# Three 256-column matmuls everywhere instead of one of 512 and one of 256, and every activation tile at 192 over a multiple of 256 bytes

## The chip, the cores and the metric

One of the eight cores of a Trainium2 chip runs the whole program. The metric is device time in microseconds (us), from three runs of the kernel before: 1252.30, 1252.81 and 1257.68 us, median 1252.81 us.

## What is computed

One decoder block on 256 tokens of width 2048, in float32. Cut to what matters here, all of its matrix products are:

```python
proj = rms_norm(x) @ w_in + b_in                 # 2048 -> q 1024, k 128, v 128, u 512, two gates of 2048
attn = sliding_window_attention(q, k, v, sinks)  # 16 heads
ssm  = glu(gelu(s5_ssm(u)) @ w_glu + b_glu)      # 512 -> 1024 -> 512
merged = sigmoid(gate_attn) * (attn @ w_branch_attn) + sigmoid(gate_ssm) * (ssm @ w_branch_ssm)
x = x + merged @ w_out                           # 2048 -> 2048
val, gate = split(rms_norm(x) @ w_up)            # 2048 -> 2 * 5632
x = x + (val * gelu(causal_conv(gate))) @ w_down # 5632 -> 2048
return rms_norm(x)
```

## The kernel before

Activations lie transposed: features on the 128 partitions, the 256 tokens along the free axis. Weights stream from memory in 416 units of 512 KB (128 partitions by 1024 floats), one after the other in the order of the blocks: q, u, kv, q, then the gates (ga, gs), the attention output (A), the GLU (glu), the branch of the state-space part (S), the output product (o), 22 blocks of the up-projection (up0 to up21) and 4 of the down-projection (dn0 to dn3). A block makes four output chunks of 128 features (m = 4) over K chunks of 128 input features; K is 16 for ga, gs, o and up, 8 for A, 4 for glu and S, 44 for dn. With m = 4 a unit holds two k steps.

**Precision by two pieces.** Weights and activations are each split into a high piece in the matmul's reduced float32 format (F32R) and a rest, also F32R. A product is made of hi*hi + hi*lo + lo*hi. `prep` does this for a unit: ScalarE casts the raw weights to `whi`, VectorE subtracts to get `wlo`. It runs five units ahead of TensorE (`LOOK`), into five buffers of each kind; four raw buffers are loaded by SyncE's queue.

**Two forms of the product.** For one weight chunk the blocks up to up0, and dn3, issue three matmuls of 256 columns: `whi` by the high activations, `whi` by the low ones, `wlo` by the high ones, all added in the same 256 columns of PSUM. Every matmul instruction loads its own weights. The blocks up1 to up21 and dn0 to dn2 (`double`) issue two: `whi` by high and low activations side by side, 512 columns into 512 columns of PSUM, and `wlo` by the high ones into the first 256. The two halves of the accumulator are added when the block is emptied: `whole` copies the second half to SBUF (ScalarE) and adds the first (VectorE), twice in each of the 21 blocks; `ev_dn` does the same twice in each of three blocks.

**Where the moving operands lie.** Each product streams an activation tile through TensorE. The tiles' addresses within a partition follow from the pools in the order in which they are opened. In the program that is built, the first tile of each kind starts at these places, given as the rest over 256 bytes:

| tile | used by | before | after the change |
|---|---|---|---|
| `A` as `xg`, later `x2g` (2048 bytes for each k: high, then low) | q, u, kv, ga, gs; up | 192 | 192 |
| `ath`, `atl` | A | 0 | 192 |
| `su` | glu | 0 | 192 |
| `sy` | S | 224 | 192 |
| `mh`, `ml` | o | 0 | 192 |
| `H` (2048 bytes for each k: high, then low) | dn | 0 | 192 |
| `whi`, `wlo` (weights) | all | 0 | 0 |

All their steps are whole multiples of 256 bytes, so the rest holds for every matmul of a block.

**What sets the order.** The kernel writes one order per engine by hand. Side work (state-space scan, attention, normalisations) stands in generators that `fill` advances when running tallies of estimated nanoseconds for each engine (`clk_pe`, `clk_v`, `clk_a`) say that there is room. TensorE's part of it (`later`) is put between the matmuls of a block by `run_aux`: attention scores, transposes and values (tile `at`), the state-space products (`pq`, `yp`), sums for the normalisations (`at<-ones,..`, `at<-dg,ones`). From ga to the A blocks there are several dozen such insertions; from the last part of A (A3y) to up0 there is none, in up0 there are two, and from up1 to the tail of dn3 there is none.

Of the kernel before, what the change touches and what calls it, by code (L numbers as in the profile page):

```python
# [8 lines left out]
F32 = mybir.dt.float32  # L9
F32R = mybir.dt.float32r  # L10
I32 = mybir.dt.int32
AF = mybir.ActivationFunctionType
ALU = mybir.AluOpType
AX = mybir.AxisListType

P = 128
T = 256
NK = 16
# [119 lines left out]
def hybrid_block_kernel(  # L138
# [14 lines left out]
    V, S = Counted(nc.vector, clk_v, dve_ns), Counted(nc.scalar, clk_a, act_ns)  # L153
    PE = Counted(nc.tensor, clk_pe, pe_ns)

    base = ctx.enter_context(tc.tile_pool(name="base", bufs=1))
# [3 lines left out]
    def open_pool(name, **kw):  # L160
        cm = tc.tile_pool(name=name, **{"bufs": 1, **kw})
        return cm, cm.__enter__()
# [20 lines left out]
    A = base.tile([P, NK, 2, T], F32R, tag="A", name="xg")  # L183
    Ah, Al = A[:, :, 0], A[:, :, 1]
    mid_cm, mid = open_pool("mid")
    X = mid.tile([P, NK, T], F32, tag="tS", name="x_in")
    ath = mid.tile([P, 8, T], F32R, tag="ath", name="ath")
    atl = mid.tile([P, 8, T], F32R, tag="atl", name="atl")
# [68 lines left out]
    def bc(ap, n):  # L257
        return ap.unsqueeze(1).to_broadcast([P, n, ap.shape[-1]])
# [18 lines left out]
        V.tensor_tensor(sq[:, 0:2], sq[:, 0:2], sq[:, 2:4], op=ALU.add)  # L277
        V.tensor_tensor(sq[:, 0], sq[:, 0], sq[:, 1], op=ALU.add)

# [1 line left out]
    V.memset(ones, 1.0)  # L281
    V.memset(eps, EPS)
    S.activation(hb[:, 0:1], eps, AF.Sqrt)
# [10 lines left out]
    warm = bank("at", P)  # L294
    for i in range(WARM):
        PE.matmul(warm, ones, ones, start=True, stop=True)
# [1 line left out]
    st = {}  # L298
    bq8 = base.tile([P, 8], F32, tag="bq8", name="bq8")

# [28 lines left out]
        ks = range(4 * b, 4 * b + 4)  # L329
        ev_proj(f"{n}{b}", acc, dst[:, 4 * b : 4 * b + 4], None, [hb[:, off + i : off + i + 1] for i in ks], AF.Tanh, 0.5)  # L330

# [1 line left out]
    def g_norm1():  # L333
        sq = mid.tile([P, 2, 4, T], F32, tag="tA", name="sq1")
        v = p1.tile([P, 2], F32, tag="sv1", name="sv1")
# [31 lines left out]
        S.copy(rs, ps[1].rearrange("p h t -> p (h t)"))  # L367
        st["rs"] = True

# [1 line left out]
    def g_ssm():  # L371
        sp = p1.tile([P, 22, NJ], F32, tag="sp", name="sp")
        ki = p1.tile([P, NJ], I32, tag="ki", name="ki")
# [252 lines left out]
        y_ev(3)  # L626
        st["y3"] = True

# [1 line left out]
    def g_attn():  # L630
        yield "D", wait_for("kv", "q0")
        qT = st["qT"]
# [88 lines left out]
    def g_norm2():  # L721
        sq, ps = st["sq"], {}
        yield "D", None
        fold(sq)

        def total():
            ps[0] = bank("at", 2)
            for h in range(2):
                PE.matmul(ps[0][:, h : h + 1], sq[:, 0, h * P : (h + 1) * P], ones[:, 0:1], start=True, stop=True)

        def spread():
            ps[1] = bank("at", 2, P)
            for h in range(2):
                PE.matmul(ps[1][:, h], ones, dg[:, h], start=True, stop=True)

        yield "D", later(total)
        n2 = mid.tile([P, 3, 2], F32, tag="ath", name="n2")
        dg = mid.tile([P, 2, P], F32, tag="atl", name="dg2")
        rstd(ps[0], n2[:, 0], n2[:, 1], n2[:, 2])
        for h in range(2):  # L740
            V.tensor_scalar(dg[:, h], ident, n2[:, 2, h : h + 1], None, op0=ALU.mult)
        yield "A", later(spread)
        st["rs2"] = base.tile([P, T], F32, tag="rs", name="rs2")
        S.copy(st["rs2"], ps[1].rearrange("p h t -> p (h t)"))
        close_pool(st["p2cm"])
        close_pool(mid_cm)
        st["ffncm"], fp = open_pool("ffn")
        st["ffn"] = fp
        st["H"] = fp.tile([P, NFF, 2, T], F32R, tag="H", name="H")
        st["gb"] = fp.tile([P, 2, T + 2], F32, tag="gb", name="gb")  # L750
        V.memset(st["gb"][:, :, 0:2], 0.0)
# [114 lines left out]
                                   in1=st["Ah"][:, k].bitcast(F32), op0=ALU.mult, op1=ALU.subtract)  # L866
        squares(d, b)

    def whole(acc, c0, out, name):
        sl = st["ffn"].tile([P, 2, T], F32, tag="xs", name=name, bufs=2)  # L870
        S.copy(sl, acc[:, c0 : c0 + 2, T : 2 * T])
        V.tensor_tensor(out, acc[:, c0 : c0 + 2, 0:T], sl, op=ALU.add)

    def ev_up(j, acc):
        rs2, fp, g = st["rs2"], st["ffn"], st["gb"]
        y = fp.tile([P, 2, T], F32, tag="cy", name=f"cy{j}")
        v = fp.tile([P, 2, T], F32, tag="cv", name=f"cv{j}")
        gd = g[:, :, 2 : T + 2]
        if j:
            whole(acc, 2, gd, f"xg{j}")  # L880
            V.tensor_tensor(gd, gd, bc(rs2, 2), op=ALU.mult)
        else:
            V.tensor_tensor(gd, acc[:, 2:4], bc(rs2, 2), op=ALU.mult)
        for i in range(2):
            c = 2 * j + i
            S.activation(y[:, i], g[:, i, 2 : T + 2], AF.Identity, bias=pcol("cb", c), scale=pcol("cw", 3 * c + 2))
        if j:
            whole(acc, 0, v, f"xv{j}")
            V.tensor_tensor(v, v, bc(rs2, 2), op=ALU.mult)
        else:  # L890
            V.tensor_tensor(v, acc[:, 0:2], bc(rs2, 2), op=ALU.mult)
        for i in range(2):
            c = 2 * j + i
            for tap in (1, 0):
                V.scalar_tensor_tensor(out=y[:, i], in0=g[:, i, tap : T + tap], scalar=pcol("cw", 3 * c + tap),
                                       in1=y[:, i], op0=ALU.mult, op1=ALU.add)
        S.activation(y, y, AF.Gelu)
        V.tensor_tensor(v, v, y, op=ALU.mult)
        split(st["H"][:, 2 * j : 2 * j + 2, 0], st["H"][:, 2 * j : 2 * j + 2, 1], v)

    def ev_dn(b, acc):
        d = st["X"][:, 4 * b : 4 * b + 4]
        V.tensor_tensor(d, d, acc[:, :, 0:T], op=ALU.add)
        for c in (0, 2):
            sl = st["ffn"].tile([P, 2, T], F32, tag="xs", name=f"xd{b}_{c}", bufs=2)
            S.copy(sl, acc[:, c : c + 2, T : 2 * T])
            V.tensor_tensor(d[:, c : c + 2], d[:, c : c + 2], sl, op=ALU.add)
        squares(d, b)
        for k in range(4 * b, 4 * b + 4):
            S.activation(st["xo"][:, k], st["X"][:, k], AF.Identity, scale=G("fin", k))  # L910
# [14 lines left out]
    def evac(name, acc):  # L925
        if name == "u":
            ev_u(acc)
        elif name == "kv":
            ev_kv(acc)
            spawn(g_attn(), dve=5000.0, act=5000.0, first=True)  # L930
        elif name[0] == "q":
            ev_q(int(name[1]), acc)
        elif name[:2] == "ga":
            if st["tA"] is None:
                st["tA"] = mid.tile([P, NK, T], F32, tag="tA", name="tA")
            ev_gate("ga", st["tA"], int(name[2]), 0, acc)
        elif name[:2] == "gs":
            if st["tS"] is None:
                st["tS"] = mid.tile([P, NK, T], F32, tag="tS", name="tS")
            ev_gate("gs", st["tS"], int(name[2]), 16, acc)  # L940
        elif name[0] == "A":
            ev_A(4 * int(name[1]) + (2 if name[-1] == "y" else 0), 2 if len(name) == 3 else 4, acc)
        elif name[0] == "S":
            ev_S(int(name[1]), acc)
        elif name[:3] == "glu":
            if name == "glu0":
                assert not gens and not aux
                close_pool(p1_cm)
                st["p2cm"], st["p2"] = open_pool("p2")
                p2 = st["p2"]  # L950
                st["mh"] = p2.tile([P, NK, T], F32R, tag="mh", name="mh")
                st["ml"] = p2.tile([P, NK, T], F32R, tag="ml", name="ml")
                st["sy"] = base.tile([P, 2, 4, T], F32R, tag="X", name="sy")
            ev_glu(int(name[3]), acc)
        elif name[0] == "o":
            ev_o(int(name[1]), acc)
        elif name[:2] == "up":
            ev_up(int(name[2:]), acc)
        elif name[:2] == "dn":
            ev_dn(int(name[2]), acc)  # L960
# [48 lines left out]
    for i, (name, K, m, k0, kw) in enumerate(units):  # L1009
# [37 lines left out]
        if name == "dn3" and i >= NU - TAIL:  # L1047
            tail.append((k0, hi, lo))
            prep(i + LOOK)
            continue  # L1050
        double = acc.shape[2] == 512 and name != "dn3"
        for kk in range(kw if double else 0):
            k = k0 + kk
            both = (st["A"] if name[0] == "u" else st["H"])[:, k].rearrange("p s t -> p (s t)")
            for c in range(m):
                PE.matmul(acc[:, c], hi[:, kk, c], both, start=k == 0, stop=False, skip_group_check=True)
                PE.matmul(acc[:, c, 0:T], lo[:, kk, c], mh[:, k], start=False, stop=k == K - 1, skip_group_check=True)
        for kk in range(0 if double else kw):
            k = k0 + kk
            for c in range(m):  # L1060
                o = acc[:, c, 0:T]
                first = k == 0 and (c % 2 == 0 or name == "dn3")
                last = k == K - 1
                PE.matmul(o, hi[:, kk, c], mh[:, k], start=first, stop=False, skip_group_check=True)
                PE.matmul(o, hi[:, kk, c], ml[:, k], start=False, stop=False, skip_group_check=True)
                PE.matmul(o, lo[:, kk, c], mh[:, k], start=False, stop=last, skip_group_check=True)
                run_aux()
            if kk == 0:
                fill()
# [21 lines left out]
        if k0 + kw == K and name == "dn2":  # L1091
            spawn(g_pre(), 2)

# [1 line left out]
    Hh, Hl = st["H"][:, :, 0], st["H"][:, :, 1]  # L1095
    Xr, xo, sq = st["X"], st["xo"], st["sq"]
    n3 = st["ffn"].tile([P, 3, 2], F32, tag="cy", name="n3")
# [141 lines left out]
```

## Time and profile before

| what | value |
|---|---|
| runs of the kernel before | 1252.30, 1252.81, 1257.68 us |
| span of the profiled execution (first to last instruction) | 1249.7 us |
| median of the runs less that span | 3.1 us |
| TensorE matmuls busy / weight loads busy | 1235.7 us (99%) / 1125.1 us (90%) |
| VectorE / ScalarE busy | 856.9 us (69%) / 620.0 us (50%) |
| mean granted TensorE clock | 0.996 |

The profiled execution's own time is its span of 1249.7 us and some 3.1 us around it, if it ran like the median. Matmuls overlap in the trace: one is shown as 276 to 284 ns long while the next starts after some 113 to 120 ns. The time that a stream of matmuls takes is therefore read from the distance between starts, or from a piece of the chain of waits divided by the matmuls in it, not from the mean duration of one. A few per cent of matmul records can be missing, so short pieces are read with care.

### The profile page before, as it was taken

To read this page: it belongs to the slowest core of one execution; us is meant where nothing else is said; L and a number is where in the kernel's file an instruction comes from. 1 tells how busy PE (TensorE), PEld (TensorE's weight loads), DVE (VectorE), ACT (ScalarE), POOL (GpSimd) and SP (SyncE) were. 2 spreads that over 40 slices of the span, in tenths; PEclk is the share of its full clock that TensorE was granted. 3 is DMA by queue.
4 is the path that set the end of the run, shared out by engine and by line. 5 is a ranking of instruction groups with operands and counts; after the bars stand their busy time and mean duration, and the time that the engine had idled before them with its cause. 6 is when DMAs were issued, how large, how long until landed. Compare 5 with 4: busy or idle time off the path is not lost.

```text
span 1249.7 us, 20901 instructions
## 1 busy us (share of the span) xinstructions
PE 1235.7 (99%) x8476; PEld 1125.1 (90%) x8476; DVE 856.9 (69%) x1220; ACT 620.0 (50%) x865; POOL 10.4 (1%) x24
## 2 busy tenths in 40 slices
PE   9999999999999999999999999999999999999996
PEld 8999899989999999988888888888888888888996
DVE  7988998989878556567677666676666755454543
ACT  7676555554444445445445454454455534343531
POOL 0000000000000000000000000000000000000000
PEclk9999999999999999999999999999999999999998
DMA  8565444444446654654655646546456475646451
GB/s 315 205 203 185 162 152 162 140 164 169 153 169 227 207 180 163 205 183 152 214 174 179 216 145 216 189 159 222 159 187 214 140 235 165 208 165 208 165 184 68
DMA packets 64896, 228.29 MB, mean 183 GB/s; under 512 B 7648, under 2 KB 9056, under 8 KB 64672
## 3 DMA queue, kind: packets, MB, share of 16 engines
q1 hardware_dynamic: 63648, 223.55, 52.9%
q0 software_dynamic: 1152, 3.41, 0.9%
q8 instruction: 66, 1.08, 0.4%
q14 instruction: 30, 0.25, 0.1%
HBM read 224.31 MB, written 2.10 MB: 181 GB/s over the span
## 4 chain that ended last, share of the span: by engine, by line
PE 98%; DVE 1%; DMA 0%; ACT 0%; SPq 0%; issue 0%; DVEq 0%
PE acc_up L132 40%; PE acc_dn L132 20%; PE acc_o L132 7%; PE acc_gs L132 7%; PE acc_ga L132 7%; PE acc_q L132 3%; PE acc_A L132 3%; PE pq L132 2%; PE at L132 2%; PE acc_u L132 2%; PE acc_S L132 2%; PE yp L132 1%; PE acc_glu L132 1%; PE aux L132 1%; DMA raw<-in_wst_dram 0%; DVE xo_sq L132 0%
## 5 line engine op out<-in xcount | busy, mean ns | idle before, releaser
L132 DVE TENSOR_TENSOR wlo<-raw,whi 128x1024 fp32r<-128x1024 f32 (+2 forms) x421 | 501.4, 1209 | 277.0 <-ACT whi L132 274.0
L132 ACT CAST whi<-raw 128x1024 fp32r<-128x1024 f32 (+2 forms) x421 | 429.5, 1038 | 420.4 <-PE acc_dn L132 111.3
L132 PE MATMUL acc_up<-x2g,whi 128*128 128x512 f32 (+1 forms) x1472 | 497.2, 387 | 0.0
L132 PE MATMUL acc_up<-x2g,wlo 128*128 128x256 f32 x1408 | 395.4, 281 | 0.0
L132 PEld LDWEIGHTS acc_up<-x2g,whi 128*128 128x128 f32 x1472 | 272.1, 188 | 62.4
L132 PEld LDWEIGHTS acc_up<-x2g,wlo 128*128 128x128 f32 x1408 | 264.3, 188 | 0.0
L132 PE MATMUL acc_dn<-H,whi 128*128 128x512 f32 (+1 forms) x856 | 245.9, 355 | 0.0
L132 PE MATMUL acc_dn<-H,wlo 128*128 128x256 f32 x692 | 194.7, 281 | 0.0
L132 PEld LDWEIGHTS acc_dn<-H,whi 128*128 128x128 f32 x856 | 150.4, 189 | 24.8
L132 PEld LDWEIGHTS acc_dn<-H,wlo 128*128 128x128 f32 x692 | 131.3, 190 | 0.0
L132 PE MATMUL acc_gs<-xg,whi 128*128 128x256 f32 x512 | 91.4, 282 | 0.0
L132 PE MATMUL acc_ga<-xg,whi 128*128 128x256 f32 x512 | 91.2, 282 | 0.0
L132 PEld LDWEIGHTS acc_gs<-xg,whi 128*128 128x128 f32 x512 | 77.8, 189 | 2.6 <-issue 1.7
L132 PEld LDWEIGHTS acc_ga<-xg,whi 128*128 128x128 f32 x512 | 77.6, 188 | 2.8 <-issue 2.0
L132 PE MATMUL acc_o<-mh,whi 128*128 128x256 f32 x256 | 72.5, 283 | 0.0
L132 PE MATMUL acc_o<-ml,whi 128*128 128x256 f32 x256 | 72.5, 283 | 0.0
L132 PE MATMUL acc_o<-mh,wlo 128*128 128x256 f32 x256 | 72.5, 283 | 0.0
L132 PE MATMUL acc_gs<-xg,wlo 128*128 128x256 f32 x256 | 71.3, 278 | 0.0
L132 PE MATMUL acc_ga<-xg,wlo 128*128 128x256 f32 x256 | 71.2, 278 | 0.0
L132 PEld LDWEIGHTS acc_o<-ml,whi 128*128 128x128 f32 x256 | 49.2, 192 | 0.0
L132 PEld LDWEIGHTS acc_o<-mh,whi 128*128 128x128 f32 x256 | 49.2, 192 | 0.0
L132 PEld LDWEIGHTS acc_o<-mh,wlo 128*128 128x128 f32 x256 | 49.2, 192 | 0.0
(212 smaller groups left out, 1371.7 us busy)
## 6 DMA issues: line engine op xcount, KB each, us to landing
raw<-in_wst_dram SPq DMA_DIRECT2D x415, 512.0 KB, 4.2
xres<-in_xT_dram POOLq DMA_DIRECT2D x1, 2048.0 KB, 9.9
x_in<-in_xT_dram SPq DMA_DIRECT2D x7, 256.0 KB, 5.9
out_dram<-xo_sq SPq DMA_DIRECT2D x7, 256.0 KB, 2.4
br<-in_ssmb_dram POOLq DMA_DIRECT2D x3, 256.0 KB, 4.2
raw<-in_wst_dram SPq DMA_DIRECT2D x2, 256.0 KB, 3.4
cT<-in_ssmc_dram SPq DMA_DIRECT2D x1, 512.0 KB, 6.3
us<-ul POOLq DMA_DIRECT2D x16, 32.0 KB, 3.1
```

Source lines behind the costliest of these rows:

```text
L132: return fn(*a, **k)
```

## The change

All blocks use three matmuls of 256 columns; the 512-column form, the accumulator's second half in use and its adding-up (`whole`, the loop in `ev_dn`) go away. VectorE now multiplies straight out of PSUM. The PSUM tiles keep their size of one 2 KB bank for each chunk, of which 256 columns are used. Two unused tiles of 48 floats (192 bytes; `room1`, `room2`) open the pools `mid` and `ffn` and so push what follows by 192 bytes; `sy` is cut out of a larger tile 56 floats (224 bytes) behind its start.

```diff
@@ pools
     mid_cm, mid = open_pool("mid")
+    mid.tile([P, 48], F32, tag="room", name="room1")
     X = mid.tile([P, NK, T], F32, tag="tS", name="x_in")
...
         st["ffn"] = fp
+        fp.tile([P, 48], F32, tag="room", name="room2")
         st["H"] = fp.tile([P, NFF, 2, T], F32R, tag="H", name="H")
...
-                st["sy"] = base.tile([P, 2, 4, T], F32R, tag="X", name="sy")
+                sy = base.tile([P, NK * T], F32R, tag="X", name="sy")[:, 56 : 56 + 8 * T]
+                st["sy"] = sy.rearrange("p (s k t) -> p s k t", s=2, k=4)
@@ emptying the accumulators
-    def whole(acc, c0, out, name):
-        sl = st["ffn"].tile([P, 2, T], F32, tag="xs", name=name, bufs=2)
-        S.copy(sl, acc[:, c0 : c0 + 2, T : 2 * T])
-        V.tensor_tensor(out, acc[:, c0 : c0 + 2, 0:T], sl, op=ALU.add)
...
-        if j:
-            whole(acc, 2, gd, f"xg{j}")
-            V.tensor_tensor(gd, gd, bc(rs2, 2), op=ALU.mult)
-        else:
-            V.tensor_tensor(gd, acc[:, 2:4], bc(rs2, 2), op=ALU.mult)
+        V.tensor_tensor(gd, acc[:, 2:4, 0:T], bc(rs2, 2), op=ALU.mult)
...
-        if j:
-            whole(acc, 0, v, f"xv{j}")
-            V.tensor_tensor(v, v, bc(rs2, 2), op=ALU.mult)
-        else:
-            V.tensor_tensor(v, acc[:, 0:2], bc(rs2, 2), op=ALU.mult)
+        V.tensor_tensor(v, acc[:, 0:2, 0:T], bc(rs2, 2), op=ALU.mult)
...
-        for c in (0, 2):
-            sl = st["ffn"].tile([P, 2, T], F32, tag="xs", name=f"xd{b}_{c}", bufs=2)
-            S.copy(sl, acc[:, c : c + 2, T : 2 * T])
-            V.tensor_tensor(d[:, c : c + 2], d[:, c : c + 2], sl, op=ALU.add)
@@ the products
-        double = acc.shape[2] == 512 and name != "dn3"
-        for kk in range(kw if double else 0):
-            k = k0 + kk
-            both = (st["A"] if name[0] == "u" else st["H"])[:, k].rearrange("p s t -> p (s t)")
-            for c in range(m):
-                PE.matmul(acc[:, c], hi[:, kk, c], both, start=k == 0, stop=False, skip_group_check=True)
-                PE.matmul(acc[:, c, 0:T], lo[:, kk, c], mh[:, k], start=False, stop=k == K - 1, skip_group_check=True)
-        for kk in range(0 if double else kw):
+        for kk in range(kw):
             k = k0 + kk
             for c in range(m):
                 o = acc[:, c, 0:T]
-                first = k == 0 and (c % 2 == 0 or name == "dn3")
+                first = k == 0 and (c % 2 == 0 or acc.shape[2] == 512)
                 last = k == K - 1
                 PE.matmul(o, hi[:, kk, c], mh[:, k], start=first, stop=False, skip_group_check=True)
                 PE.matmul(o, hi[:, kk, c], ml[:, k], start=False, stop=False, skip_group_check=True)
```

TensorE's order at the border from up0 to up1, before the change (`acc_up_6054` is up0's accumulator, `acc_up_6341` up1's; `x2` stands for two instructions alike):

```order
L132 MATMUL acc_up_6054<-x2g,whi_6141 128x256 x2
L132 MATMUL acc_up_6054<-x2g,wlo_6142 128x256
L132 MATMUL acc_up_6341<-x2g,whi_6184 128x512
L132 MATMUL acc_up_6341<-x2g,wlo_6185 128x256
L132 MATMUL acc_up_6341<-x2g,whi_6184 128x512
```

And with the change (`acc_up_6343` is up1's):

```order
L132 MATMUL acc_up_6055<-x2g,whi_6142 128x256 x2
L132 MATMUL acc_up_6055<-x2g,wlo_6143 128x256
L132 MATMUL acc_up_6343<-x2g,whi_6185 128x256 x2
L132 MATMUL acc_up_6343<-x2g,wlo_6186 128x256
L132 MATMUL acc_up_6343<-x2g,whi_6185 128x256 x2
```

Each `whi` row of 512 columns becomes two of 256 at the same place, 1344 times in up1 to up21 and 528 times in dn0 to dn2; nothing else changes its place on TensorE.

VectorE where block up1 is emptied, before:

```order
L132 TENSOR_TENSOR gb<-acc_up_6341,xg_6520 128x2x256
L132 TENSOR_TENSOR gb<-gb,rs_6235 128x2x256
L132 TENSOR_TENSOR cv_6519<-acc_up_6341,xv_6526 128x512
L132 TENSOR_TENSOR cv_6519<-cv_6519,rs_6235 128x512
L132 SCALAR_TENSOR_TENSOR cy_6518<-gb,pr,cy_6518 128x256 x4
```

And with the change:

```order
L132 TENSOR_TENSOR wlo_6579<-raw_6462,whi_6578 128x1024
L132 TENSOR_TENSOR gb<-acc_up_6343,rs_6236 128x2x256
L132 TENSOR_TENSOR cv_6585<-acc_up_6343,rs_6236 128x512
L132 SCALAR_TENSOR_TENSOR cy_6584<-gb,pr,cy_6584 128x256 x4
L132 TENSOR_TENSOR cv_6585<-cv_6585,cy_6584 128x512
```

Two of VectorE's instructions go in each block (48 in all with dn0 to dn2), and with them 48 copies on ScalarE (`xg`, `xv`, `xd`). One weight cast of ScalarE changes places with a neighbour; SyncE's and GpSimd's orders stay.

## The prediction

> **What bounds the kernel now.** I read the page's first two parts, then the chain of waits, then the timeline of TensorE in the stages that the change touches.
>
> ```profile
> span 1249.7 us, 20901 instructions
> PE 1235.7 (99%) x8476; PEld 1125.1 (90%) x8476; DVE 856.9 (69%) x1220; ACT 620.0 (50%) x865; POOL 10.4 (1%) x24
> PEclk9999999999999999999999999999999999999998
> PE 98%; DVE 1%; DMA 0%; ACT 0%; SPq 0%; issue 0%; DVEq 0%
> ```
>
> The chain that ended last is TensorE for 98% of the span, at full granted clock. So the time is the number of matmuls times their pace, and only the pace can change it. "99% busy" says nothing of the pace. The chain in order of time does: a piece's time over its count.
>
> ```profile
> 63.03 11.90 PE acc_q L132 x105
> 74.93 0.22 PE at L132 x2
> 75.15 4.24 PE acc_q L132 x36
> 86.46 6.01 PE acc_ga L132 x51
> 363.15 8.64 PE acc_glu L132 x72
> 383.81 11.60 PE acc_S L132 x96
> 395.41 92.15 PE acc_o L132 x768
> 502.60 482.71 PE acc_up L132 x2757
> 985.31 241.27 PE acc_dn L132 x1512
> ```
>
> All the matmuls of the first seven rows but the two of `at` have 256 columns, and there are three paces:
> - **quick**, 113.3 ns: 11.90 / 105 on tile `xg` (192 over 256 bytes);
> - **middle**, 117.8 ns: 4.24 / 36 and 6.01 / 51, same tile, same shape, after two other matmuls came between;
> - **slow**, 120.0 ns: 8.64 / 72 and 92.15 / 768, tiles `su`, `mh`, `ml` (0 over 256).
>
> S, at 224, runs at about 119 (11.60 us less the first one after a stall, over 95, is somewhat above). Nothing but the tile's place separates the 768 matmuls of o from those of q and ga: shape, weights' place and clock are the same. So I read the slow pace as due to place 0, and place 192 as having two paces.
>
> Of the shape that goes, the groups by form give the price:
>
> ```profile
> L132 PE MATMUL acc_up<-x2g,whi 128*128 128x512 f32 x1344 | 474.9, 397 | 0.0
> L132 PE MATMUL acc_dn<-H,whi 128*128 128x512 f32 x528 | 186.6, 399 | 0.0
> ```
>
> One of 512 is shown longer (397 ns) than the distance to the next, so its busy time covers the pair of 512 and 256: 474.9 / 1344 = 353.4 ns, 186.6 / 528 = 353.4 ns. Three of 256 take 340.0 at the quick pace, 353.4 at the middle one and 360.0 at the slow one. **The change gains 13.4 ns for each of 1872 triples at the quick pace, nothing at the middle, and loses 6.6 at the slow.** Each ns of pace is worth 1872 x 3 = 5.6 us.
>
> **Which pace the new stretch gets.** Block up0 already has the new form, on the very tile (`x2g`, 192). Its timeline shows starts of `wlo` matmuls, one for each triple:
>
> ```profile
> 487.99 0.28 PE L132 MATMUL acc_up<-x2g,wlo 128*128 128x256 f32 x1
> 496.49 0.28 PE L132 MATMUL acc_up<-x2g,wlo 128*128 128x256 f32 x1
> 496.60 0.50 PE L132 MATMUL at<-ones,sqA 128*128 128x1 f32 x4
> 497.64 0.28 PE L132 MATMUL acc_up<-x2g,wlo 128*128 128x256 f32 x1
> 501.52 0.28 PE L132 MATMUL acc_up<-x2g,wlo 128*128 128x256 f32 x1
> 502.00 0.27 PE L132 MATMUL at<-dg,ones 128*128 128x128 f32 x1
> 502.68 0.28 PE L132 MATMUL acc_up<-x2g,wlo 128*128 128x256 f32 x1
> 510.16 0.28 PE L132 MATMUL acc_up<-x2g,wlo 128*128 128x256 f32 x1
> ```
>
> Between the first two rows are 25 triples: 8.50 / 75 = 113.3. After the first insertion 11 triples take 3.88 us: 117.6. After the second, 22 triples take 7.48 us: 113.3. So the pace holds while nothing comes between, and each of these two insertions changes it over; the two together leave it as it was. Behind them up1 to the tail of dn3 has no insertion, nor has the way from S to up0. The pace in which S leaves its one stall therefore decides some 850 us:
>
> ```profile
> 381.31 1.22 DVE wlo L132
> 382.53 1.14 DVE tS L132
> 383.67 0.14 issue
> ```
>
> TensorE waits there until VectorE has emptied an accumulator of S. This wait stays; when it ends against TensorE's own beat is not in the profile. I bound the pace by the nearest rows: of the 39 streams of eight or more matmuls on `xg` between two insertions, 22 are quick and 17 middle; the first and last whole pieces are
>
> ```profile
> 12.96 2.72 PE acc_q L132 x24
> 287.71 6.01 PE acc_gs L132 x51
> ```
>
> (113.3 and 117.8). I take quick, by that majority and because up0, the one place where a stream came out of tiles at 0 to a tile at 192, began quick.
>
> **The change part by part**, quick pace, middle in brackets:
> 1. o: 768 x (120.0 - 113.3) = 5.1 us (1.7).
> 2. S: 192 x about 5.6 = 1.1 us (0.2); its stall stays.
> 3. A and glu: 480 matmuls, 3.2 us (1.1). Insertions cut A, so both paces will mix: 2.0 us.
> 4. up0: nothing (0.5 us lost, since its quick and middle stretches, some 147 and 41 matmuls, would change places).
> 5. up1 to up21: 1344 x 13.4 ns = 18.0 us (0).
> 6. dn0 to dn2: 528 x 13.4 ns = 7.1 us (0).
> 7. dn3 with its tail, already three of 256: 176 x 20.0 ns = 3.5 us (1.2).
>
> Sum 36.8 us (3.7). q to gs don't change; their mix of paces is open from run to run, 256 + 256 triples of ga and gs at 13.4 ns being 6.9 us from end to end, which may be why the runs differ by 5.4 us.
>
> 8. The adding-up that goes: 42 + 6 copies on ScalarE and as many additions on VectorE.
>
> ```profile
> L132 ACT COPY xg<-acc_up 128x512 f32<-128x512 f32 x21 | 12.1, 578 | 0.0
> L132 DVE TENSOR_TENSOR cv<-acc_up,xv 128x512 f32<-128x512 f32 x21 | 14.5, 691 | 34.2 <-ACT xv L132 34.2
> ```
>
> Some 27 us of ScalarE and 33 us of VectorE (with `xv`, `xg` and `xd`), all beside TensorE: worth nothing. If TensorE waited for an emptied accumulator they would be worth up to 2.5 us a block, but two accumulators alternate and each has a whole block of 21.7 us.
>
> 9. A quicker TensorE eats a unit of 24 matmuls in 2.72 us instead of 2.83. ScalarE's cast (1.05 us) and VectorE's subtraction (1.22 us) fit, and the supply has been faster:
>
> ```profile
> 10.00:40.00 30.00, 29.80 (x262) 29.80 (x263) 27.88 (x62) 23.83 (x33) 0.00 (x0) 1.00 0.92 339
> 47.00:74.00 27.00, 27.00 (x241) 27.00 (x240) 25.41 (x64) 16.08 (x24) 0.00 (x0) 1.00 0.61 201
> 600.00:980.00 380.00, 380.00 (x2153) 330.05 (x2152) 258.20 (x304) 189.53 (x236) 0.00 (x0) 1.00 0.55 184
> ```
>
> 512 KB in 2.72 us is 193 GB/s; the second row held the quick pace at 201 GB/s with VectorE and ScalarE busier than in up, at clock 1.00. Should a unit come late, the stream would stop and draw its pace anew.
>
> The third weight load in a triple shows in those rows too: weight loads are busy for 330 of 380 us in up and for all of 27 us in q at the quick pace, so they fill TensorE's load side without setting the pace there.
>
> Two rules of the Trainium skill speak against the change. "TensorE: Matmul & The Clock Gate", section Back-to-back issue gap, gives N/2.4 + 2.5 ns a matmul; by that a pair is 325.0 and a triple 327.5 ns, an estimate of 4.7 us more for 1872. The rows disagree: 256 columns never took less than 113.3 ns. The same page, section Step-by-step: what each phase is for, says that loading the next weights takes no SBUF read bandwidth from the running matmul, which has two read ports. By that rule the tile's place should not matter; the rows of q against o speak against it, though they don't prove the place.
>
> **Rivals.**
> - **Middle pace from S on** (same place, the other draw): 3.7 us gained, 1252.8 - 3.7 = 1249.1. For it: 17 of 39. Against: up0 began quick.
> - **The place is not the cause**, something else about tile `A` is: A to o stay, dn0 to dn2 lose 528 x 6.6 = 3.5, dn3 stays, up gains 18.0. 1238.3. Against: `x2g` and `H` have the same steps, so little but the place is left.
> - **Slower: a third matmul costs a full slow one.** Three at 120.0 in up and dn, as in o: 1872 x 6.6 = 12.4 us more, 1265.2; it decides from a pace above 117.8 on. For it: o and dn3 ran so for 92 us and 63 us on end. Against: no stream on `xg` of any length did, up0 included.
> - **The pace changes over on the way** through a late unit or a boundary between blocks: between 1216 and 1249, by where. Against: it held over q's 105, and the pair's 353.4 over all of up.
>
> **How the numbers follow.** The sum is made on the profiled execution, 1249.7 - 36.8 = 1212.9 us of span, and 3.1 us around it: 1216.0, which is the median less the sum. Its own range is 1211 to 1222 (A, the mix in q to gs, and the sum's roundings). Chances: quick 0.60, middle 0.22, changing over 0.07, place not the cause 0.06, slower 0.05. The middle case can't be left out of eight in ten, so the range is 1211 to 1251. What differs from no change by over 0.5% (6.3 us) can be told here: faster 0.60 + 0.07 + 0.06 = 0.73, same 0.22, slower 0.05.
>
> **What would show it.** In the chain: `acc_o` at 87 us for 768 and no slow pieces behind gs; `acc_up` as one piece of some 457 us for 4032 matmuls behind up0, `acc_dn` with the tail near 240 us. If up takes 475 us with o at 90.5, it is the middle pace; if o stays at 92, the place was not the cause. A forecast wrong in sign needs a pace above 117.8 ns in up or a wait of TensorE that isn't there now. Starts 117.6 ns apart behind 510 us would make it wrong at once.

## The result, and the profile after

The change takes 1219.26 us (median of four runs, 1214.48 to 1220.22) against 1252.55 us (four runs, 1251.32 to 1257.68): a ratio of 0.9729, 95% interval 0.9699 to 0.9759. The forecast was 1216.0 us, 1211 to 1251. Two executions among all those below, one of the places alone (2303.52 us) and one of the kernel before (1502.66 us), ran far slower for a reason that stays open; they are in no comparison.

The page of the changed kernel, then its chain of waits in order of time (start, us, what; the count is of matmuls):

```profile
span 1218.4 us, 24557 instructions
PE 1204.8 (99%) x10348; PEld 1181.8 (97%) x10348; DVE 825.9 (68%) x1172; ACT 600.2 (49%) x817; POOL 10.4 (1%) x24
PEclk9999999999999999999999999999999999999998
PE 98%; DVE 1%; DMA 0%; ACT 0%; SPq 0%; issue 0%; DVEq 0%
```

```profile
361.65 8.48 PE acc_glu L132 x72
382.11 11.54 PE acc_S L132 x96
393.66 90.45 PE acc_o L132 x768
484.11 9.54 PE acc_up L132 x81
499.49 464.80 PE acc_up L132 x4101
964.29 231.20 PE acc_dn L132 x2040
```

TensorE still is the whole chain, at full clock. The weight loads went from 90% to 97% busy. They fill the whole time at the quick pace (220.00 of 220 us from 970 us on) and at the slow one (80.00 of 80 us in o before), so their busy share does not tell whether they set the pace. What differs is pace. Behind up0's insertions, 4101 matmuls take 464.80 us: 113.3 ns, quick, where 482.71 us stood for the pairs (both pieces hold the last 69 matmuls of up0, which had the quick pace before too). dn's long piece falls from 241.27 to 231.20 us, 113.3 ns each, its last part (dn3) having been slow. But o is at 90.45 / 768 = 117.8 ns: middle, not quick, and so are glu and S.

The start of up0 is middle too (9.54 us for 81, 9.20 before). Its timeline, `wlo` matmuls (one for each triple) around the two insertions:

```profile
492.66 0.28 PE L132 MATMUL acc_up<-x2g,wlo 128*128 128x256 f32 x1
493.37 0.28 PE L132 MATMUL acc_up<-x2g,wlo 128*128 128x256 f32 x1
493.49 0.50 PE L132 MATMUL at<-ones,sqA 128*128 128x1 f32 x4
494.17 0.28 PE L132 MATMUL acc_up<-x2g,wlo 128*128 128x256 f32 x1
498.41 0.28 PE L132 MATMUL acc_up<-x2g,wlo 128*128 128x256 f32 x1
498.89 0.61 PE L132 MATMUL at<-dg,ones 128*128 128x128 f32 x4
499.91 0.28 PE L132 MATMUL acc_up<-x2g,wlo 128*128 128x256 f32 x1
508.41 0.28 PE L132 MATMUL acc_up<-x2g,wlo 128*128 128x256 f32 x1
```

Two triples in 0.71 us ahead of the sums (0.355 each), twelve in 4.24 us behind them (0.353), 25 in 8.50 us behind `at<-dg,ones` (0.340). So the sums left a middle stream middle. The prediction had every insertion change the pace over; by that, up0's rest and all of up would have gone middle, quick, middle. The time came out right, and one of its reasons was false: S left its stall at the middle pace, and up was quick all the same. The experiments ask what the place does, and what the insertions do.

### The profile page after: what moved, and what is told of

It reads as the page before. It is cut to its first block, busy times and chain, and to the rows that moved or that the text cites. A ratio compares the mean times of both kernels' runs of the same rounds, so it can differ in the third digit from the quotient of the medians.

```text
span 1218.4 us, 24557 instructions
## 1 busy us (share of the span) xinstructions
PE 1204.8 (99%) x10348; PEld 1181.8 (97%) x10348; DVE 825.9 (68%) x1172; ACT 600.2 (49%) x817; POOL 10.4 (1%) x24
## 4 chain that ended last, share of the span: by engine, by line
PE 98%; DVE 1%; DMA 0%; ACT 0%; SPq 0%; issue 0%; DVEq 0%
PE acc_up L132 39%; PE acc_dn L132 19%; PE acc_gs L132 7%; PE acc_ga L132 7%; PE acc_o L132 7%; PE acc_q L132 3%; PE acc_A L132 3%; PE pq L132 2%; PE at L132 2%; PE acc_u L132 2%; PE acc_S L132 2%; PE yp L132 1%; PE acc_glu L132 1%; PE aux L132 1%; DMA raw<-in_wst_dram 0%; DVE xo_sq L132 0%
## 5 line engine op out<-in xcount | busy, mean ns | idle before, releaser
L132 PE MATMUL acc_up<-x2g,whi 128*128 128x256 f32 x2816 | 479.6, 276 | 0.0
L132 PEld LDWEIGHTS acc_up<-x2g,whi 128*128 128x128 f32 x2816 | 424.2, 188 | 0.0
L132 PE MATMUL acc_up<-x2g,wlo 128*128 128x256 f32 x1408 | 388.8, 276 | 0.0
L132 PE MATMUL acc_dn<-H,whi 128*128 128x256 f32 x1384 | 235.7, 276 | 0.0
L132 PEld LDWEIGHTS acc_dn<-H,whi 128*128 128x128 f32 x1384 | 208.3, 188 | 0.0
L132 PE MATMUL acc_dn<-H,wlo 128*128 128x256 f32 x692 | 191.1, 276 | 0.0
L132 PEld LDWEIGHTS acc_ga<-xg,wlo 128*128 128x128 f32 x256 | 48.1, 188 | 0.0
L132 PEld LDWEIGHTS acc_gs<-xg,wlo 128*128 128x128 f32 x256 | 48.1, 188 | 0.0
```

The costliest lines, as they stand in the source:

```text
L132: return fn(*a, **k)
```

## The experiments

Two theories of the gain stood against each other at first: the place of the moving tile sets the pace of 256-column streams, or something else about tile `A` and the shape does. Then came two questions behind the first: place by itself or distance from the weights, and whether insertions set the pace.

**Three matmuls of 256 everywhere, all places as before.**

```diff
-    mid.tile([P, 48], F32, tag="room", name="room1")
...
-        fp.tile([P, 48], F32, tag="room", name="room2")
...
-                sy = base.tile([P, NK * T], F32R, tag="X", name="sy")[:, 56 : 56 + 8 * T]
-                st["sy"] = sy.rearrange("p (s k t) -> p s k t", s=2, k=4)
+                st["sy"] = base.tile([P, 2, 4, T], F32R, tag="X", name="sy")
```

> Three matmuls of 256 everywhere, all tiles where they lay before. If the place decides, up runs its triples on x2g (192) in 340 ns, 18.0 us less, and dn0 to dn2 on H (0) in 360 ns, 3.5 us more: 1238 us. If the shape alone made the gain, dn runs quick as well: 1252.6 - 18.0 - 7.1 - 3.5 = 1224 us, and little of the change is left for the places.

1237.28 us (1237.11 to 1237.90, four runs), ratio 0.9884 (0.9869 to 0.9898). Its chain:

```profile
396.12 92.15 PE acc_o L132 x768
503.31 464.80 PE acc_up L132 x4101
968.11 244.78 PE acc_dn L132 x2040
```

up is as quick as with the whole change; o and dn, at 0, run at 92.15 / 768 = 244.78 / 2040 = 120.0 ns. The shape by itself brings up's 18 us and costs dn 3.5; the places bring the rest. These runs also lie within 0.8 us of each other, those of the change within 5.7.

**The places alone, 512 columns kept.**

```diff
+    mid.tile([P, 48], F32, tag="room", name="room1")
...
+        fp.tile([P, 48], F32, tag="room", name="room2")
...
-                st["sy"] = base.tile([P, 2, 4, T], F32R, tag="X", name="sy")
+                sy = base.tile([P, NK * T], F32R, tag="X", name="sy")[:, 56 : 56 + 8 * T]
+                st["sy"] = sy.rearrange("p (s k t) -> p s k t", s=2, k=4)
```

> The kernel before with the two 192-byte tiles and sy's shift, and the 512-column form kept. If the place of the moving tile sets the pace of the 256-column streams, o falls from 92.2 us to between 87 (quick) and 90.5 (middle), dn3 from 360 ns a triple to 340 or 353, and up stays at 353.4 ns a pair: 1241 to 1249 us against 1252.6. If the place is not the cause, o and dn3 stay at 120.0 ns a matmul and the time at 1252 to 1253. What a pair of 512 and 256 takes on H at 192 is open; x2g at 192 makes 353.4 likely.

Four runs of 1241.81 to 1246.98 us, ratio 0.9939 (0.9917 to 0.9962). The profile is of one more execution, of 1245.84 us:

> Places alone once more, for a profile at full clock (the first one's fell to half of it). With H at 192, dn3 (three of 256) at 340 or 353 ns a triple and o at 87 to 90.5 us; the pair of 512 and 256 in dn0 to dn2 at 353.4 ns if H at 192 does as x2g does in up.

```profile
392.25 90.45 PE acc_o L132 x768
498.08 482.71 PE acc_up L132 x2757
980.79 240.27 PE acc_dn L132 x1512
```

```profile
L132 PE MATMUL acc_dn<-H,whi 128*128 128x512 f32 x528 | 186.6, 397 | 0.0
```

o went from 120.0 to 117.8 ns by its place alone, and dn's piece is 1.0 us shorter by dn3 at 117.8. Of the 5.6 us between the spans of this profile and that of before, 1.8 are an earlier start of A (304.60 against 306.39 us), which q to gs gave by their mix of paces. The pair of 512 and 256 takes 186.6 / 528 = 353.4 ns on H at 192, just as at 0 before and as on x2g: it had the same price at both places. So neither part alone gives dn its 7 us: it took the shape and the place together.

**The weights at 192 too.**

```diff
     raws, arrive = {}, {}
+    strm.tile([P, 48], F32, tag="room", name="room0")
...
-    mid.tile([P, 48], F32, tag="room", name="room1")
...
-        fp.tile([P, 48], F32, tag="room", name="room2")
```

The new tile opens the pool of the weight buffers and pushes all pools behind it, so that the activation tiles stay where the change has them.

> As the change, but the weight buffers whi and wlo also lie at 192 over 256 bytes, so that every activation tile is at distance 0 from them. If the distance between moving tile and weights counts, all streams run slow, 120.0 ns, q to gs too: some 10 + 4 + 28 + 14 us more, about 1275 us. If the place of the moving tile counts by itself, nothing changes: 1214 to 1221 us, up's triples at 340 ns.

1275.51 us (two runs, 0.1 us apart), ratio 1.0188 (1.0168 to 1.0208).

```profile
406.44 92.16 PE acc_o L132 x768
514.24 492.12 PE acc_up L132 x4101
1006.36 244.80 PE acc_dn L132 x2040
```

Every activation tile lies at 192, as in the change, and every stream runs at 120.0 ns: 492.12 / 4101 = 244.80 / 2040. The change's gain is gone and 23.5 us more (1251.97 us for the kernel before beside it). up's piece alone is 27 us dearer than with the weights at 0. So the moving tile's place alone does not decide.

**The weights at 64.** Only 16 floats open the weights' pool, and the two rooms of the change stay, so that what follows lies at 0:

```diff
     raws, arrive = {}, {}
+    strm.tile([P, 16], F32, tag="room", name="room0")
```

> As the change, with the weights at 64 and ath, atl, su, mh, ml, H at 0 (distance 192 from the weights), tile A and sy staying at 192 (distance 128). If the distance decides, o and dn run quick or middle although their tiles lie at 0 (o 87 to 90.5 us, dn 340 or 353 ns a triple), and q to gs and up run at the 118.7 to 120 ns that distance 128 had in the last round: up about 505 us; 1250 to 1265 us in all. If the place itself decides (0 slow, 192 quick), up keeps 340 ns, dn takes 360 and o 92.2 us: 1237 us. If weights off a multiple of 256 are what is slow, all runs at 120: about 1275 us.

1254.51 us (eight runs, 1254.02 to 1255.02), ratio 1.002 (1.0009 to 1.0032).

```profile
400.78 87.04 PE acc_o L132 x768
503.31 486.66 PE acc_up L132 x4101
989.97 240.27 PE acc_dn L132 x2040
```

o streams tiles at 0, the slow place so far, and is quick: 87.04 / 768 = 113.3 ns. x2g at 192, the quick place so far, takes 486.66 / 4101 = 118.7 ns. dn on H at 0 takes 117.8. The pace goes with the distance from the weights, that is the moving tile's start less the weights' start, modulo 256 bytes: 192 here for o and dn, 128 for up. (That it repeats after 256 bytes was taken for granted: the steps inside these tiles are multiples of 512 bytes, 128 weights or 256 tokens of 4 bytes, and no run was made to tell the two.) (My 505 us for up was a slip: 4101 at 118.7 to 120 ns are 487 to 492.)

**Other distances.** Weights at 0, tile A at 192, the two rooms resized (and sy cut at 64 and 128 in the first two):

```diff
-    mid.tile([P, 48], F32, tag="room", name="room1")
+    mid.tile([P, M], F32, tag="room", name="room1")   # M, N = 16, 16; 32, 32; 40, 56; 24, 8
...
-        fp.tile([P, 48], F32, tag="room", name="room2")
+        fp.tile([P, N], F32, tag="room", name="room2")
```

> As the change, but ath, atl, su, sy, mh, ml and H at 64 over 256 bytes, the weights at 0; tile A stays at 192, so up keeps 340 ns a triple. If the distance counts in both directions alike, 64 does as 192: o 87 to 90.5 us, dn 340 or 353 ns a triple, 1214 to 1221 us. If only a moving tile 64 bytes ahead of the next multiple of 256 escapes the weights, o is 92.2 us and dn 360 ns a triple as at 0: about 1237 us.

> As before with these tiles at 128, the farthest distance there is in 256. If the distance counts by its size, 128 is at least as good as 192: o 87 to 90.5 us, dn 240 us or less, 1219 us or less. If 192 alone is good: o 92.2 us, dn 360 ns a triple, about 1237 us.

> As the change, with ath, atl, su, mh, ml at 160 and H at 224, weights at 0. So far distance 0 gave 120.0 ns, 192 gave 113.3 or 117.8, 64 gave 117.8 and 128 gave 118.7 to 120. If the pace follows steps of 64 bytes, 160 lies between 128 and 192 and 224 between 192 and 0, as S had it at 224 before (119 ns): o near 91 us, dn near 242 us, 1226 to 1230 us. If a finer step counts, one of them may run below 113.3 ns.

> The same at 96 and 32. By steps of 64, 96 lies between 64 (117.8) and 128 (118.7 to 120), 32 between 0 (120.0) and 64 (117.8): o 90.5 to 92 us, dn 240 to 244 us, 1226 to 1237 us. A pace below 117.8 ns at either would show that 192 is not the only distance with a quick state.

They took 1228.25, 1233.31, 1228.66 and 1228.71 us (two runs each). The rows of their chains, in the same order, o (first pool) and dn (second):

```profile
393.44 90.45 PE acc_o L132 x768
964.07 240.26 PE acc_dn L132 x2040
```

```profile
395.33 92.16 PE acc_o L132 x768
967.31 242.08 PE acc_dn L132 x2040
```

```profile
392.88 90.11 PE acc_o L132 x768
962.65 241.39 PE acc_dn L132 x2040
```

```profile
393.34 92.14 PE acc_o L132 x768
965.33 238.00 PE acc_dn L132 x2040
```

Time over count, with the other runs' rows:

| distance, bytes mod 256 | ns for one of 256 columns | from |
|---|---|---|
| 0 | 120.0 | o, dn with three alone; all with the weights at 192 |
| 32 | 116.7 | dn |
| 64 | 117.8 | o, dn |
| 96 | 120.0 | o |
| 128 | 120.0; 118.7 | o; dn, and up with the weights at 64 |
| 160 | 117.3 | o |
| 192 | 113.3 or 117.8 | up, dn, o |
| 224 | 118.3 | dn |

Of these eight only 192 reached 113.3 ns, but by the sign that the last forecast had named, a pace below 117.8 ns, 32 (116.7) and 160 (117.3) stand out as well. Two paces were seen at 128 too (118.7 and 120.0). 64 did not do as 192: H at 64 came straight out of a quick up and ran at 117.8. In steps of 64 the order is not one of size either: 128 is worse than 64. Of the four forecasts only that for 160 and 224 held. At 64 and 128 the times fell between the two that had been written down, and at 96 and 32 dn was quicker (238.00 us) than its 240 to 244. The change's place is the best of those tried; finer steps and other tiles' layouts were not tried.

**What an insertion does.** Behind `at<-dg,ones` in up0, the two sums once more:

```diff
+        def again():
+            ps[2] = bank("at", 2)
+            for h in range(2):
+                PE.matmul(ps[2][:, h : h + 1], sq[:, 0, h * P : (h + 1) * P], ones[:, 0:1], start=True, stop=True)
+
+        yield "A", later(again)
+        st["rs2"] = rs2
```

> As the change, with the two small sum matmuls (at<-ones,sqA) once more behind at<-dg,ones in up0, results unused. If such an insertion sets the pace of what follows (the sums to middle, dg to quick, whatever came before), everything from there to dn3's tail runs at 117.8 ns: up 475 us, dn near 249, some 27 us more, 1245 to 1247 us. If the pace is a draw at each stop, or long streams find the quick pace by themselves, 1219 us in some runs or all, with up's triples at 340 ns.

1246.41 us (1243.36 to 1247.10, four runs), ratio to before 0.9951 (0.9935 to 0.9967): 27 us more than the change, for two small matmuls (four instructions in the trace) that take 0.34 us.

```profile
497.96 0.61 PE L132 MATMUL at<-dg,ones 128*128 128x128 f32 x4
498.64 0.28 PE L132 MATMUL acc_up<-x2g,wlo 128*128 128x256 f32 x1
500.69 0.28 PE L132 MATMUL acc_up<-x2g,wlo 128*128 128x256 f32 x1
500.81 0.50 PE L132 MATMUL at<-ones,sqA 128*128 128x1 f32 x4
```

```profile
500.97 0.34 PE at L132 x4
501.30 480.64 PE acc_up L132 x4080
981.94 240.27 PE acc_dn L132 x2040
```

Six triples in 2.05 us behind `at<-dg,ones` (0.342, quick), then 480.64 / 4080 = 117.8 ns to the end of up and 117.8 in dn: middle for 720 us. Nothing on the way changed it over: no unit's border, no block's, no emptied accumulator. That an insertion changes the pace over is refuted by the change's profile, where the sums left a middle stream middle. That the sums always leave the middle pace is not true either. The same two insertions also stand in the first normalisation, near 40 us, on `xg` at distance 192. The piece behind the sums there, in the kernel before and in the second profile of the change (shown further down):

```profile
43.44 2.47 PE acc_u L132 x21
```

```profile
43.94 2.38 PE acc_u L132 x21
```

117.6 ns and 113.3. And in up0 of the kernel with its tiles at 160 and 224:

```profile
492.02 0.50 PE L132 MATMUL at<-ones,sqA 128*128 128x1 f32 x4
492.71 0.28 PE L132 MATMUL acc_up<-x2g,wlo 128*128 128x256 f32 x1
497.13 0.28 PE L132 MATMUL acc_up<-x2g,wlo 128*128 128x256 f32 x1
497.25 0.61 PE L132 MATMUL at<-dg,ones 128*128 128x128 f32 x4
```

13 triples in 4.42 us behind the sums, 0.340 each: quick. In the eleven profiles used here that have tile A at distance 192, the sums of both normalisations came 23 times and left the middle pace 16 times and the quick one 7 times; in five of the seven TensorE had been held up at the sums (0.46 to 0.61 us for the four instructions, where they otherwise take 0.34). `at<-dg,ones` came 22 times and left the quick pace each time, 15 times out of the middle and 7 times out of the quick one. So `at<-dg,ones` sets the quick pace as far as these profiles go; the sums mostly leave the middle one, and what decides behind them is open.

**The draw at S's stall.** Two more: the change again, and the change with a pair of the kind of `at<-dg,ones` behind the first unit after the stall.

```diff
+        if name == "S2" and k0 == 0:
+            pulse = bank("at", 2, P)
+            for h in range(2):
+                PE.matmul(pulse[:, h], ones, ident, start=True, stop=True)
```

> The change once more, beside the kernel with the extra pair in S. If S to up0 takes whichever pace the stall leaves and all else is set, the runs spread over some 6 us: 945 matmuls at 4.5 ns are 4.2 us, and q to gs add theirs; the profile has o at either 87.0 or 90.5 us and up behind at<-dg,ones at 340 ns a triple either way. If up is drawn too, some runs lie near 1245 us.

> As the change, with two extra 128-column float32 matmuls of the kind of at<-dg,ones (ones by the identity, result unused) in S, after the first unit behind its stall, 0.45 us. If that insertion sets the quick pace whatever came before, the rest of S, o and the first part of up0 always run at 113.3 ns, o 87.0 us: 1214 to 1216 us in every run. If the quick pace behind at<-dg,ones has another reason (its place in up0, the tile x2g), o stays at 90.5 us in some runs, and the times spread from 1214 to 1221 us as with the change.

The change: 1214.65, 1215.12, 1214.84, 1218.59 and 1219.34 us, ratio 0.9720 (0.9705 to 0.9735). Its profile, of the execution of 1214.65 us, differs from the first one where it was expected:

```profile
381.26 11.13 PE acc_S L132 x96
392.40 87.04 PE acc_o L132 x768
494.45 464.80 PE acc_up L132 x4101
```

o is quick here and was middle there; up is quick in both. Of the nine runs of the change four lie from 1214.48 to 1215.12 and five from 1218.59 to 1220.22, nothing between. With the extra pair: 1216.82, 1216.04, 1216.28, 1214.45, ratio 0.9711 (0.9698 to 0.9724), none in the upper group. Three of the four lie just above the 1214 to 1216 us of the forecast. That none is in the upper group fits a set pace, but S was quick in its profile already ahead of the pair, so whether the pair set it is not shown; and the median is no better than that of the change beside it, so no gain of the pair is shown either.

## Why the prediction was right, and where not

- **The price of a triple** (340.0, 353.4, 360.0 ns, and 353.4 for the pair) held to the tenth of a ns, also on tiles where it had not been seen. up gained 17.9 us (18.0 forecast), dn0 to dn3 with the tail 10.3 (7.1 + 3.5).
- **"I read the slow pace as due to place 0"**: the places gave what was forecast, but the cause named was too narrow. With the weights moved, tiles at 192 were slow and tiles at 0 quick: the distance from the weights counts. The table of the places left that open, since the weights lay at 0 in both kernels.
- **"Each of these two insertions changes it over" failed.** From one quick-middle-quick in up0 I took a switch. In the runs `at<-dg,ones` left the quick pace every time, whatever came before, and the sums mostly the middle one. So the step after it, "the pace in which S leaves its one stall therefore decides some 850 us", was wrong: the stall decides the 945 matmuls to up0's first insertion, about 4.2 us, and the 696 us behind up0's insertions (464.80 + 231.20) were quick whether S had left its stall quick or middle. That up came out quick as forecast was luck as far as this step goes: by the step as written, the middle S of the profiled execution would have made up and dn middle. The rival of the middle pace (1249 us, 0.22) had up and dn in it and did not come about that way in any run; the extra sums brought it about, at 1246.
- **The sum.** 36.8 us forecast, 31.3 between the two profiles' spans. The term that was mis-sized is o: 1.7 us instead of 5.1. A, glu and S together, from A's first matmul to o's, gave 1.4 instead of 3.1, and up0 lost 0.35: nearly all middle in that execution. up and dn fell short by 0.4, and q to gs, counted as nothing, gave 0.4. (S before ran at 118.4 ns, 8.41 us for 71 matmuls, and not at 119.) The execution of 1214.65 us, span 1212.9, has the 36.8 us to the tenth of a us, its o quick; but its A blocks also began 1.2 us earlier (305.16 against 306.39), which q to gs, the same in both kernels, gave by their mix of paces; so the agreement is partly chance.
- **What was added around the span**, 3.1 us, came from the median and not from the profiled execution. In the profiles since it is 1.8 us (1220.22 less 1218.4). With the same 1.8 us, the profiled execution of before took some 1251.5 us, below its median; this is an estimate.
- **The draw**: 22 to 17 for the quick pace was counted over insertions of all kinds. For the stall in S the nine runs of the change say four to five, if the two groups of times are o's two paces, as they are in the two that have a profile.
- **Adding-up at no price and the supply of weights**: as forecast. VectorE lost 31 us of busy time and ScalarE 20 (33 and 27 had been counted), and no wait of TensorE appeared. That the weight loads do not set the pace was argued and is not shown: they are busy all the time at 113.3 and at 120.0 ns alike.
- **The two rules of the Trainium skill.** By the formula of the Trainium skill, page "TensorE: Matmul & The Clock Gate", section Back-to-back issue gap, the triple was to be dearer than the pair by an estimated 2.5 ns; the section gives the formula for a matmul in isolation, and not for a stream that loads weights for each. The triple was cheaper by 13.4 ns at the quick pace, equal at the middle one and dearer by 6.6 at a distance of 0. The same page of the Trainium skill, section Step-by-step: what each phase is for, states that loading weights takes no read bandwidth from the running matmul. The prediction drew from it that the tile's place should not matter, and that does not hold here: moving nothing but the weight pool's start by 192 bytes took up from 113.3 to 120.0 ns. Whether read bandwidth is what is lost, no run here shows.

## What to carry to other kernels

Where TensorE is the whole chain, divide pieces of the chain by their counts before believing "99% busy": a stream of float32r matmuls of 256 columns, each with its own weight load, ran at 113.3 to 120.0 ns by where its two operands lay modulo 256 bytes and, at a distance of 192, by which of two paces it had come into. 192 bytes of padding took 1.5% off (1237.28 to 1219.26 us) at the activations and put 4.6% on (to 1275.51) when the weights moved along. The best distance of those tried was moving less stationary = 192. Measure it as a distance: with both operands at 192 the pace was that of both at 0. If a pace has two states, ask what sets it before estimating chances: two tiny matmuls cost 27 us here, and one quick-middle-quick could be a switch as well as two settings. A setting, too, has to be counted over many instances: the sums left the middle pace in 16 of 23.

## What was not expected of the hardware

At a distance of 192 a stream has one of two paces and keeps it, in one execution for 720 us and more than 6000 matmuls, through every border between blocks (480.64 us for 4080 and 240.27 for 2040, both 117.8 ns). What ran last ahead of it bears on which one it gets: quick 22 times of 22 behind `at<-dg,ones`, middle 16 times of 23 behind the sums. Why this is so, and why the distance between the two operands counts, the runs don't show. The pair of 512 and 256 had 353.4 ns wherever it was seen (x2g at 192, H at 0 and at 192), just the middle pace of three of 256.
